# The second mixture of experts on four experts at a time, and the place of its spill branch

## The chip, the cores and the metric

The program runs on one core of a Trainium2 chip: TensorE (matrix products, PE in the profile), VectorE (DVE), ScalarE (ACT), GpSimd (POOL) and SyncE (SP), which issues most DMAs; 16 DMA engines move the data. The metric is the device time of one execution in microseconds (us); the median of several runs counts.

## The reference, cut to what matters

A two-layer backbone over 256 latent and 256 context tokens of 1024 values, all in float32. Layer 0 has a convolution and attention mixer, layer 1 a recurrent one (RG-LRU); each layer ends with a mixture of 16 experts in 4 groups. In layer 1 only the latent tokens go on, so the second mixture has 256 tokens:

```python
def hier_moe(h, w_grp, b_grp, w_rt, b_rt, w_gate, w_up, w_down):
    g_logit = jnp.einsum('bsd,dg->bsg', h, w_grp, preferred_element_type=f32) + b_grp.astype(f32)
    p_grp = jax.nn.softmax(g_logit, axis=-1)
    g_idx = jnp.argmax(g_logit, axis=-1)
    ...
    top_v, top_i = lax.top_k(e_sel, TOP_K)                       # two of the four experts of the group
    w_sel = jax.nn.softmax(top_v, axis=-1) * p_sel
    ...
    hg = jnp.einsum('bsd,edf->bsef', h, w_gate)                  # 16 experts, 1024 -> 512
    hu = jnp.einsum('bsd,edf->bsef', h, w_up)
    act = jax.nn.silu(hg) * hu * gate[..., None].astype(h.dtype)
    return jnp.einsum('bsef,efd->bsd', act, w_down)              # 512 -> 1024, summed over the experts
```

Each token uses two experts, so the kernel multiplies an expert's weights only with the tokens that chose it.

## The kernel before

**Weights.** SBUF holds 23 buffers of 1 MiB, the units (`NU`). The list `todo` has all weight tiles (1,024 KB each) in the order of use; `load_ahead(n)` (L119) issues their DMAs on SyncE so that up to n tiles are loaded or loading ahead of use, as long as units are free; `wtile` takes the next tile, `used` gives its unit back. A unit given back goes to the end of a queue and the oldest is taken first; a DMA into it waits until the last reader of its old contents is done. An expert has six tiles: gate (`wg`) and up (`wu`) in two halves of the contraction, down (`wd`) in two halves of the outputs. `w_first` and `w_second` (L287, L292) append them for a list of experts. Both mixtures read all 16 experts: 96 tiles each.

**First mixture** (`moe0`, L997; 512 tokens). Groups of four experts are worked at once: `four` (L1098) holds the tokens of each expert as 32 stationary columns, so that four products of 32 columns stand side by side, and goes through `NR` = 3 parts of 32 slots. The rows come by indirect DMA (`fetch`) and go back by indirect DMA (`scatter`) into the DRAM tile `z`, except those of the last group, which stay on the chip (`yl`) and are placed by products with one-hots (`own`). The choice's weight is multiplied into the activations (L1150).

**Second mixture** (`moe1`, L1212; 256 tokens in two blocks of 128, each expert with 64 slots, `CAP1`). It works on eight pairs of experts. `first(pr)`: `slots_of` (L928) builds, for 2 x 64 slots, the one-hot `Sl` and the weighted one-hot `Sw` on VectorE; `gather_slots` (L945) multiplies the tokens with `Sl` (fp32, 16 products of 128 columns); `Sw` is transposed and split into two fp32r parts; `slots_by` (L891) multiplies with gate and up weights, 64 stationary columns per expert, two experts side by side; `act_of` makes the activations. `second(pr)`: four transposes of the activations, the down products, and for each half of the outputs and each token block three fp32r products with the split `Sw` (`mm3`, L176), which add into four PSUM banks `acc` over all pairs. Then the gated sum (`add_gated`, L534) and the store.

**Order.** The lines above give the program order. Within a window the scheduler of the framework moves an instruction forward on its engine when its inputs are ready by a cost model, so the trace shows for instance combining products of one pair among the down products. DMAs keep the order of SyncE's queue.

**Spill.** If more tokens choose an expert than it has slots, `spill_rounds` (L954) works them off in a loop inside a branch (`tc.If`) on a count `nri` made by `route`. With these inputs the count is zero, so its body isn't run, but each engine reads the count and branches, and nothing is scheduled across the branch. Its body names five to eight units. It stands behind the second group of the first mixture (L1177) and behind the fifth pair of the second (L1259). Before it `load_ahead(8)` keeps the number of loads lower, so that units are left for the body; behind it 12 or 13 are allowed again.

## Time and profile before

| | us |
|---|---|
| median of 3 runs | 1070.16 (1069.8 to 1070.17) |
| profiled execution | 1069.07 |
| its span, first to last instruction | 1067.3 |
| first mixture, first gate product to the last down product | 342.4 to about 605 |
| second mixture, first gate product to the end | 816.0 to 1067.3 |
| mean granted clock of TensorE over the span | 0.960 of 2.4 GHz |

All times in the views are from the start of the span. Busy times are sums over instructions, so an engine that is busy for all of a stretch may still be the one that is not waited for; the lists of waits say which.

### The profile page before, as it was taken

The numbers are of one execution on the slowest core, as the hardware profiler recorded it, in microseconds if no ns is written. First come the engines' busy times: TensorE is split into PE (matmuls) and PEld (weight loads), VectorE is DVE, ScalarE is ACT, GpSimd is POOL, SyncE is SP. The second block draws the span as 40 slices with busy tenths as digits, with TensorE's granted clock in tenths as the row PEclk, the third lists the DMA queues.
The fourth block names the chain that finished last, engine by engine and source line by source line (L and its number), as shares of the span: only waits on it lengthen the run. The fifth ranks groups of instructions, "written<-read, shape, count | busy, mean of one in ns | idle before, by whom it ended". The sixth has DMA issues, their size and how long they took to land. (4 is left out here: it accounts for less than half of the span.)

```text
span 1067.3 us, 15108 instructions
## 1 busy us (share of the span) xinstructions
PE 972.1 (91%) x6153; PEld 544.2 (51%) x6153; DVE 457.3 (43%) x957; ACT 269.6 (25%) x487; POOL 188.1 (18%) x152
## 2 busy tenths in 40 slices
PE   4699999999987999999999989888576999999997
PEld 2488657556876333333433478656363444443342
DVE  3756565567464020110202388798974111221112
ACT  3622433423121010000101254585721101100010
POOL 0244010031033011010010336467410000000000
PEclk9699999999997999999999999999777999999999
DMA  9934866879576899979999911242775999997941
GB/s 366 377 112 154 347 238 245 314 278 418 212 280 248 335 385 401 420 278 392 420 420 413 369 41 41 79 157 80 295 304 224 422 421 418 414 423 271 422 169 39
DMA packets 49548, 310.65 MB, mean 291 GB/s; under 512 B 7528, under 2 KB 8296, under 8 KB 14912
## 3 DMA queue, kind: packets, MB, share of 16 engines
q1 hardware_dynamic: 45648, 301.63, 71.0%
q0 software_dynamic: 3824, 7.99, 2.0%
q8 instruction: 50, 0.82, 0.3%
q14 instruction: 26, 0.21, 0.1%
HBM read 304.28 MB, written 9.50 MB: 294 GB/s over the span
## 5 line engine op out<-in xcount | busy, mean ns | idle before, releaser
L899 PE MATMUL ba<-w,hgT 128*64 128x512 f32 x512 | 112.7, 594 | 0.0
L178 PE MATMUL bz<-hT,wsp 128*128 128x256 f32 (+1 forms) x224 | 76.9, 345 | 0.0
L179 PE MATMUL bz<-hT,wsp 128*128 128x256 f32 (+1 forms) x224 | 74.5, 334 | 0.9 <-DVE hT L158 0.7
L180 PE MATMUL bz<-hT,wsp 128*128 128x256 f32 (+1 forms) x224 | 73.9, 331 | 0.0
L899 PEld LDWEIGHTS ba<-w,hgT 128*64 128x64 f32 x512 | 36.3, 137 | 70.0 <-issue 69.8
L899 PE MATMUL ba<-w,actT 128*64 128x512 f32 x256 | 66.9, 601 | 4.1 <-DVE actT L233 2.7
L1106 PE MATMUL bz<-w,hgT 128*32 128x512 f32 x512 | 61.4, 593 | 0.2 <-PEq L961 0.2
L155 ACT ACTIVATE wsp<-w 128x512 fp32r<-128x512 f32 (+1 forms) x64 | 46.5, 781 | 59.4 <-PE bz L180 17.4
L1106 PE MATMUL ba<-w,hgT 128*32 128x512 f32 x512 | 61.2, 592 | 0.0
L158 POOL TENSOR_TENSOR wsp<-w,wsp 128x512 fp32r<-128x512 f32 (+1 forms) x19 | 40.8, 2153 | 91.1 <-ACT wsp L155 81.5
L158 DVE TENSOR_TENSOR wsp<-w,wsp 128x512 fp32r<-128x512 f32 (+1 forms) x49 | 48.0, 1010 | 13.3 <-ACT wsp L155 13.0
L911 DVE TENSOR_TENSOR act<-ba,silu 128x512 f32<-128x512 f32 x8 | 5.5, 691 | 105.9 <-PE ba L899 105.9
L388 PE MATMUL bz<-w,sT 128*32 128x512 f32 x384 | 46.0, 604 | 3.8 <-DMA w<-in_ada_w_dram 3.8
L1340 DVE SCALAR_TENSOR_TENSOR uc<-u,ocw,uc 128x510 f32<-128x510 f32 (+2 forms) x48 | 44.5, 984 | 4.1 <-POOL uc L1338 4.0
L178 PEld LDWEIGHTS bz<-hT,wsp 128*128 128x128 f32 x224 | 42.1, 189 | 7.6 <-ACT wsp L155 3.3
L179 PEld LDWEIGHTS bz<-hT,wsp 128*128 128x128 f32 x224 | 42.3, 189 | 4.7 <-DVE hT L158 0.9
L1106 PE MATMUL ba<-w,actT 128*32 128x512 f32 x384 | 44.6, 593 | 0.0
L1106 PE MATMUL bz<-w,actT 128*32 128x512 f32 x384 | 44.4, 593 | 0.0
L180 PEld LDWEIGHTS bz<-hT,wsp 128*128 128x128 f32 x224 | 42.3, 189 | 3.6
L179 PE MATMUL bz<-wsp,hT 128*128 128x512 f32 x96 | 39.1, 407 | 3.4 <-DVE wsp L158 3.4
L873 ACT ACTIVATE ys<-ba 128x512 fp32r<-128x512 f32 (+1 forms) x24 | 12.6, 525 | 116.9 <-PE ba L899 107.9
L178 PE MATMUL bz<-wsp,hT 128*128 128x512 f32 x96 | 38.5, 408 | 2.4 <-ACT hT L155 2.4
(371 smaller groups left out, 1690.5 us busy)
## 6 DMA issues: line engine op xcount, KB each, us to landing
w<-in_wg_dram SPq DMA_DIRECT2D x64, 1024.0 KB, 11.4
w<-in_wu_dram SPq DMA_DIRECT2D x64, 1024.0 KB, 11.7
w<-in_wd_dram SPq DMA_DIRECT2D x64, 1024.0 KB, 11.1
w<-in_ada_w_dram SPq DMA_DIRECT2D x48, 1024.0 KB, 6.9
w<-in_od_w_in_dram SPq DMA_DIRECT2D x8, 1024.0 KB, 4.9
w<-in_w_qkv_dram SPq DMA_DIRECT2D x6, 1024.0 KB, 10.3
w<-in_w_conv_dram SPq DMA_DIRECT2D x6, 1024.0 KB, 7.8
w<-in_ev_w_out_dram SPq DMA_DIRECT2D x4, 1024.0 KB, 10.0
```

The costliest lines, as they stand in the source:

```text
L155: S.activation(hi, src, AF.Copy)
L158: (eng or lo_engine()).tensor_sub(lo, src, hi.bitcast(F))
L178: T.matmul(o, l[0], r[0], start=start, stop=False)
L179: T.matmul(o, l[0], r[1], start=False, stop=False)
L180: final[0] = T.matmul(o, l[1], r[0], start=False, stop=stop)
L388: T.matmul(m[32 * j:32 * j + 32], sT[:, k], w[:, j * 512:(j + 1) * 512], start=(k == 0), stop=(k == KD - 1), tile_position=(0, 32 * j))
L873: S.activation(dst[0], p, AF.Copy)
L899: T.matmul(o[i * n:(i + 1) * n], actT[:, k0 + k, i * n:(i + 1) * n], w[:, k], start=(k0 + k == 0), stop=(k0 + k == nk - 1))
L911: V.tensor_mul(t, up, s)
L1106: T.matmul(o[r][32 * j:32 * j + 32], actT[r][:, k0 + k, 32 * j:32 * j + 32], ws[j][:, k], start=(k0 + k == 0), stop=(k0 + k == nk - 1), ti ...
L1340: V.scalar_tensor_tensor(c[:, :, j:256], src[:, :, 0:256 - j], tap, c[:, :, j:256], op0=ALU.mult, op1=ALU.add)
```

## The change

The second mixture is rebuilt on the helpers of the first: `four`, the activations' transposes and the tables of slots (`slot_rows`) move out of `moe0` and take the number of parts as an argument. `moe1` now works on four groups of four experts, 32 columns each, in two parts (`NR1` = 2; 64 slots per expert as before). The tokens are split into two fp32r parts `hp` once (`in_parts`), and the gather of a group is 32 fp32r products of 256 columns with one-hots `S` (`rows_of`). The choice's weight goes into the activations (`tg`), so that the combining products use plain one-hots (`own`), which are one part: two products instead of three per part, half and block, and no transposes of `Sw`. The weights' order becomes four gate tiles, four gate, eight up, eight down per group. The combining products of a group's second half are issued behind the next group's gate products (`later`).

In both mixtures the spill branch moves behind the last group's up products and transposes, ahead of its down products; the `load_ahead(8)` and the return to 12 or 13 go. In `moe0` the one-hot for the first gather comes from `rows_of` instead of from `ats` and `gr`, and the load of the square-root table is tied to the last copy instead of the last SiLU. Small tiles are allocated by size so that both mixtures share them (`per_block`).

```diff
-SPILL0 = 1
-SPILL1 = 4
+NR1 = 2
+CAP1 = 32 * NR1
...
-    slot1 = cst.tile([128, 2, 64], F, name="slot1")
+    slot1 = cst.tile([128, 4, 32], F, name="slot1")
...
-    w_first(1, [0, 1])
-    for e in range(0, NE, 2):
-        if e < NE - 2:
-            w_first(1, [e + 2, e + 3])
-        w_second(1, [e, e + 1])
+    for q in range(4):
+        w_first(1, range(4 * q, 4 * q + 4))
+        w_second(1, range(4 * q, 4 * q + 4))
...
+    def rows_of(S, key, nb, q, rs, tmp):
+        for m, r in enumerate(rs):
+            V.tensor_scalar(tmp, key, -float(4 * q * BIG + 32 * r), None, op0=ALU.add)
+            for b in range(nb):
+                t = S[:, b, 128 * m:128 * m + 128]
+                V.tensor_scalar(t, slot1.rearrange("p a b -> p (a b)"), tmp[:, 0, b:b + 1], None, op0=ALU.is_equal)
+                V.scalar_tensor_tensor(t, slot1.rearrange("p a b -> p (a b)"), tmp[:, 1, b:b + 1], t.bitcast(F),
+                                       op0=ALU.is_equal, op1=ALU.add)
+
+    def four(place, nr, rows, nk, get):
+        o = [place([128, 512]) for _ in range(nr)]
+        for k0 in range(0, nk, 4):
+            ws = [get(j, k0) for j in range(4)]
+            for r in range(nr):
+                for k in range(4):
+                    for j in range(4):
+                        T.matmul(o[r][32 * j:32 * j + 32], rows(r, k0 + k)[:, 32 * j:32 * j + 32], ws[j][:, k],
+                                 start=(k0 + k == 0), stop=(k0 + k == nk - 1), tile_position=(0, 32 * j))
+            used(*ws)
+        return o
...
     def moe0(h2, ts, lg, rest, h2d):
...
+        rows_of(own, key, NT, 0, [0], view(small([128, 16], "ks"), [128, 2, NT]))
...
+            at = transposed_act(bank8, act)
             if q == 3:
+                spill_rounds(0, CAP0, NT, again, key, w, nri, empty)
                 give(hg01, hgT01, ys01)
...
-            if q == SPILL0 - 1:
-                load_ahead(8)
-            if q == SPILL0:
-                spill_rounds(0, CAP0, NT, again, key, w, nri, empty)
-                load_ahead(12)
-        warm(AF.Sqrt, silu[0])
+        warm(AF.Sqrt, final[1])
...
     def moe1(h2, ts, lg, rest):
         nb = 2
         load_ahead(13)
+        hp = [unit([128, 2, D], "hp", R) for _ in range(2)]
+        def in_parts(b):
+            for i in range(2):
+                c = slice(512 * i, 512 * i + 512)
+                split(hp[0][:, b, c], hp[1][:, b, c], h2[b][:, c], V)
+        in_parts(0)
         goh, ef, pos, key, w, nri = route(nb, lg, CAP1)
         rest()
+        in_parts(1)
+        give(*ts)
+        ks = view(small([128, 16], "ks"), [128, 2, nb])
+        hgT = unit([128, KD, 256], "hgT")
+        def gather(q):
+            S = piece([128, nb, 256], "S", R)
+            rows_of(S, key, nb, q, range(NR1), ks)
+            for k in range(0, KD, 2):
+                p = bank([128, 2, 256])
+                for i in range(2):
+                    for b in range(nb):
+                        for m, h in enumerate(hp):
+                            T.matmul(p[:, i], h[:, b, (k + i) * 128:(k + i + 1) * 128], S[:, b],
+                                     start=(b + m == 0), stop=(b + m == nb))
+                evict(hgT[:, k:k + 2], p)
+        gather(0)
+        tp = slot_rows(nb, NR1, goh, ef, pos, w)
...
+        def add(q, h, own, y):
+            for b in range(nb):
+                for n in range(2 * NR1):
+                    T.matmul(acc[b][h], own[:, n // 2, b], y[:, n // 2, n % 2],
+                             start=(q + n == 0), stop=(q == 3 and n == 2 * NR1 - 1))
+        later = lambda: None
+        for q in range(4):
+            g = four(bank, NR1, rows, KD, lambda j, k0: wtile(("wg", 1, 4 * q + j, k0)))
+            later()
+            sl = [piece([128, 512], "silu") for _ in range(NR1)]
+            for r in range(NR1):
+                S.activation(sl[r], g[r], AF.Silu)
+            u = four(bank, NR1, rows, KD, lambda j, k0: wtile(("wu", 1, 4 * q + j, k0)))
+            act = [piece([128, 512], "act") for _ in range(NR1)]
+            for r in range(NR1):
+                n = NR1 * q + r
+                V.scalar_tensor_tensor(act[r], u[r], tg[:, n:n + 1], sl[r], op0=ALU.mult, op1=ALU.mult)
+            if q < 3:
+                gather(q + 1)
+            else:
+                gates = gate_rows(1, 5, 1)
+            at = transposed_act(bank, act)
+            if q == 3:
+                spill_rounds(1, CAP1, nb, whole, key, w, nri)
+            own = piece([128, NR1, nb, 128], "own", R)
...
+            yh = [ys, ys if q < 3 else unit([128, NR1, 2, 512], "ys", R)]
+            o = [None, None]
+            for h in range(2):
+                o[h] = four(bank, NR1, at, 4, lambda j, k0: wtile(("wd", 1, 4 * q + j, h)))
+                if h == 0:
+                    for r in range(NR1):
+                        put_parts((yh[0][:, r, 0], yh[0][:, r, 1]), o[0][r])
+            add(q, 0, own, yh[0])
+            for r in range(NR1):
+                put_parts((yh[1][:, r, 0], yh[1][:, r, 1]), o[1][r])
...
```

`slot_rows` is the code that stood in `moe0` (L1009 to L1039) with the number of blocks and parts as arguments; it fills `tp`, from which `tg` (the weight of each slot) and `last` (its token) come.

## Rows read from the trace of the kernel before

**Rows 1.** The page, its parts 1 and 2: busy time of TensorE (us, share of the span, instructions), then what the DMA engines moved in each of the 40 slices of 26.7 us, in GB/s.

```profile
PE 972.1 (91%) x6153; PEld 544.2 (51%) x6153; DVE 457.3 (43%) x957; ACT 269.6 (25%) x487; POOL 188.1 (18%) x152
...
GB/s 366 377 112 154 347 238 245 314 278 418 212 280 248 335 385 401 420 278 392 420 420 413 369 41 41 79 157 80 295 304 224 422 421 418 414 423 271 422 169 39
```

**Rows 2.** Busy time of each engine in the stretches of two pairs of experts of the second MoE (from one pair's first gate product to the next pair's): the stretch, its length, busy us and instructions of PE, PEld, DVE, ACT and POOL, granted TensorE clock, DMA share, GB/s. The second stretch holds the spill branch.

```profile
895.28:925.84 30.56, 29.87 (x147) 13.15 (x147) 5.91 (x16) 2.88 (x6) 0.00 (x0) 1.00 1.01 419
...
956.61:989.64 33.03, 30.73 (x147) 13.26 (x146) 6.30 (x18) 2.77 (x5) 0.00 (x0) 1.00 0.76 299
```

**Rows 3.** The same view in a stretch of 10 us near the end.

```profile
1030.00:1040.00 10.00, 9.72 (x47) 3.26 (x43) 0.69 (x1) 1.20 (x2) 0.00 (x0) 1.00 0.00 0
```

**Rows 4.** Who waited for whom between 816 and 1067 us: the longest wait of TensorE by total (total us, times, longest us).

```profile
PE bz L178 <- ACT ys L873: 3.2, 5, 0.7
```

**Rows 5.** TensorE's instructions in order of time (start us, us from the first start to the last end, engine, line, operation, names, shapes, count): gather products, gate and up products, and the down products of a pair with the combining products among them, until the next gather.

```profile
829.91 3.84 PE L951 MATMUL ba<-S,h 128*128 128x128 f32 x32
...
833.90 13.96 PE L899 MATMUL ba<-w,hgT 128*64 128x512 f32 x64
...
849.18 4.50 PE L899 MATMUL ba<-w,actT 128*64 128x512 f32 x18 [0.74 <-ACT actT L231]
853.61 0.73 PE L178 MATMUL bz<-ys 128*128 128x512 f32 x2
...
859.13 1.16 PE L951 MATMUL ba<-S,h 128*128 128x128 f32 x8
```

**Rows 6.** The same view in the first MoE: transposes of activations and the down products on 32 columns.

```profile
386.85 0.60 PE L1158 MATMUL ba<-ident,act 128*128 128x128 f32 x4
387.29 0.60 PE L1158 MATMUL bz<-ident,act 128*128 128x128 f32 x4
387.82 3.64 PE L1106 MATMUL ba<-w,actT 128*32 128x512 f32 x32
391.27 3.62 PE L1106 MATMUL bz<-w,actT 128*32 128x512 f32 x32
```

**Rows 7.** The same view: two fp32r products of 256 columns in the recurrent mixer, then two of 512 columns in its output projection.

```profile
690.14 0.28 PE L179 MATMUL bz<-hT,wsp 128*128 128x256 f32 x1
690.26 0.28 PE L180 MATMUL bz<-hT,wsp 128*128 128x256 f32 x1
...
788.06 0.39 PE L179 MATMUL ba<-wsp,mixT 128*128 128x512 f32 x1
788.29 0.40 PE L180 MATMUL ba<-wsp,mixT 128*128 128x512 f32 x1
```

**Rows 8.** The DMA queue of SyncE in order of time (issues of the second MoE's weights, 1,024 KB each), and from the view of the DMA queues the gates' loads (KB each, median us from issue to landing).

```profile
793.76 11.12 SPq L126 DMA_DIRECT2D w<-in_wd_dram  x3
...
820.13 6.77 SPq L126 DMA_DIRECT2D w<-in_wg_dram  x4
...
971.33 4.60 SPq L126 DMA_DIRECT2D w<-in_wd_dram  x4
...
gates<-rows SPq DMA_DIRECT2D x6, 512.0 KB, 14.3
```

**Rows 9.** Busy time and clock in stretches of 5 us around the second MoE's first products (columns as in rows 2).

```profile
810.00:815.00 5.00, 4.53 (x26) 4.50 (x27) 4.09 (x18) 0.81 (x2) 0.00 (x0) 0.62 0.04 16
...
820.00:825.00 5.00, 5.00 (x26) 1.68 (x24) 0.00 (x0) 0.60 (x1) 0.00 (x0) 1.00 0.85 316
```

**Rows 10.** All engines in order of time at that place: the last operation on `key`, the first one-hot comparison, the first of 32 gather products, the first gate products.

```profile
808.95 0.16 DVE L858 SCALAR_TENSOR_TENSOR key<-key,pos 128x4 f32<-128x4 f32 x1
...
809.15 0.28 DVE L938 TENSOR_SCALAR S<-slot,key 128x128 f32<-128x128 f32 x1
...
810.74 1.16 PE L951 MATMUL ba<-S,h 128*128 128x128 f32 x4
...
816.03 13.96 PE L899 MATMUL ba<-w,hgT 128*64 128x512 f32 x64
```

**Rows 11.** All engines in order of time at the end: the last down products, and the subtraction that makes the second part of their result.

```profile
1056.33 2.79 PE L899 MATMUL ba<-w,actT 128*64 128x512 f32 x10
...
1059.79 0.69 DVE L874 TENSOR_TENSOR ys<-ba,ys 128x512 fp32r<-128x512 f32 x1 [1.33 <-ACT ys L873]
```

**Rows 12.** Two groups of four experts of the first MoE (columns as in rows 2; the second begins right behind its spill branch), and from the waits of SyncE's queue its own time at the branch lines.

```profile
408.44:474.46 66.02, 66.02 (x617) 23.80 (x609) 6.93 (x10) 6.57 (x11) 6.01 (x6) 1.00 0.92 382
474.46:541.67 67.21, 67.06 (x617) 25.28 (x616) 7.79 (x11) 5.97 (x10) 2.92 (x3) 1.00 0.96 391
...
SPq L961 <- SPq L961: 6.0, 4, 3.7
```

**Rows 13.** All engines in order of time at the end of the first MoE: reads of the scattered rows, their sums on GpSimd, the first product that needs one.

```profile
583.10 4.34 SPq L1191 DMA_DIRECT2D zb<-z  x8
...
589.91 10.03 POOL L1194 TENSOR_TENSOR zb<-zb 128x512 f32<-128x512 f32 x8 [46.07 <-DMA zb<-z]
...
607.03 1.02 PE L1204 MATMUL ba<-zb,ident 128*128 128x512 f32 x2
```

**Rows 14.** The modulation products at the start of the kernel, in order of time, and the busy time and clock of a stretch of 5 us there (columns as in rows 2).

```profile
26.91 1.06 PE L388 MATMUL bz<-w,sT 128*32 128x512 f32 x8 [1.41 <-DMA w<-in_ada_w_dram]
29.41 1.93 PE L388 MATMUL bz<-w,sT 128*32 128x512 f32 x8 [1.43 <-DMA w<-in_ada_w_dram]
...
30.00:35.00 5.00, 2.43 (x12) 0.71 (x4) 2.30 (x13) 2.06 (x4) 0.00 (x0) 0.50 0.80 214
```

More of the change, by code (lines that the diff above doesn't have):

```diff
@@ L997, in moe0, with transposed_act @@
+    def transposed_act(place, act):
+        at = [piece([128, 4, 128], "actT") for _ in act]
+        for t, c in zip(at, act):
+            p = place([128, 4, 128])
+            for k in range(4):
+                T.transpose(p[:, k], c[:, k * 128:(k + 1) * 128], ident)
+            evict(t, p)
+        return lambda r, k: at[r][:, k]
     def moe0(h2, ts, lg, rest, h2d):
@@ L1130, in moe0 @@
             rows_T(r)
-        last = small([128, NR, NT], "last")
+        last = view(small([128, 16], "last"), [128, NR, NT])
         for r in range(NR):
@@ L1141, in moe0 @@
                     fetch(q + 1, r)
-            g = four(hgT, KD, lambda j, k0: wtile(("wg", 0, 4 * q + j, k0)))
+            g = four(bank8, NR, lambda r, k: hgT[r][:, k], KD, lambda j, k0: wtile(("wg", 0, 4 * q + j, k0)))
             sl = [piece([128, 512], "silu") for _ in range(NR)]
@@ new lines, in moe1, with whole @@
+        gather(0)
+        tp = slot_rows(nb, NR1, goh, ef, pos, w)
+        last = view(small([128, 16], "last"), [128, 4 * NR1, nb])
+        tg = small([128, 16], "tg")[:, 0:4 * NR1]
+        for b in range(nb):
+            V.tensor_scalar(last[:, :, b], tp[:, :, 0], float(BIG - 128 * b), None, op0=ALU.add)
+        V.tensor_copy(tg, tp[:, :, 2])
+        ys = unit([128, NR1, 2, 512], "ys", R)
+        acc = [[bank([128, 512], "z") for _ in range(2)] for _ in range(nb)]
+        def whole():
+            t = unit([128, 2, D], "h2")
+            for b in range(nb):
+                V.tensor_add(t[:, b], hp[0][:, b].bitcast(F), hp[1][:, b].bitcast(F))
+            return [t[:, b] for b in range(nb)], [t]
@@ new lines, in rows, with later @@
+        def rows(r, k):
+            return hgT[:, k, 128 * r:128 * r + 128]
+        def add(q, h, own, y):
+            for b in range(nb):
+                for n in range(2 * NR1):
[22 more added lines that the diff above has]
+            for r in range(NR1):
+                for b in range(nb):
+                    n = NR1 * q + r
+                    V.tensor_scalar(own[:, r, b], slot0, last[:, n, b:b + 1], None, op0=ALU.is_equal)
+            yh = [ys, ys if q < 3 else unit([128, NR1, 2, 512], "ys", R)]
[6 more added lines that the diff above has]
+            add(q, 0, own, yh[0])
+            for r in range(NR1):
+                put_parts((yh[1][:, r, 0], yh[1][:, r, 1]), o[1][r])
+            def later(q=q, own=own, y=yh[1]):
+                add(q, 1, own, y)
@@ L1263, in decay_rates @@
+        for h in range(2):
+            if h:
+                later()
+            hs = slice(h * 512, (h + 1) * 512)
+            for b in range(nb):
+                add_gated(b, h, acc[b][h], gates[:, 0])
+                nc.sync.dma_start(out[0, b * 128:(b + 1) * 128, hs], xb(b)[:, hs])
     def decay_rates(after):
```

157 lines of the change are left out of this document (52 added, 105 removed).

## The prediction

> **What bounds the kernel now.** The page first [rows 1]: TensorE is busy for 91% of the span, and in the second MoE (slices 32 to 40) the DMA engines move about 420 GB/s in nearly every slice, so two resources look full. Which of them sets the pace is read from three views. One pair of experts takes 30.6 us, of which TensorE is busy for 29.9 [rows 2]. A pair's weights are 12 tiles of 1,024 KB (1.049 MB); at the 419 GB/s of that row a tile takes 2.50 us, the same that lies between two products that wait for their tiles at the start of the kernel (26.91 to 29.41) [rows 14], and a pair 30.0 us. So the two are within 2% of each other, but the waits decide: no wait of TensorE on a transfer stands in the list, its longest is 3.2 us on ScalarE [rows 4]. The DMA engines rest three times in this stage: before the first weights come free (0.04 busy at 810 to 815) [rows 9], around the spill branch (0.76 over that pair) [rows 2], and at the end: from 1030 on nothing is moved while TensorE still multiplies for 30 us [rows 3, 11]. TensorE is the bound; the transfers would be done earlier.
>
> **The order of products, counted.** An fp32 product is two instructions. Now, a pair's gate and up products are 64 instructions on 64 columns and take 13.9 us [rows 5], so 27.8 for two pairs. After, a group's four experts are 128 + 128 instructions on 32 columns, and the first MoE has just this form: 32 instructions every 3.44 us [rows 6], 8 x 3.44 = 27.5. So the columns themselves gain nothing (the slots are the same 64 per expert, in two parts of 32). The down half is 128 instructions, 13.8 us for the group; now it takes 849.18 to 859.13 = 9.95 us for a pair with six combining products in it [rows 5]. At 0.218 us an instruction and 0.23 a combining product [rows 7] these are 32 x 0.218 + 6 x 0.23 = 8.4; the 1.6 left over, with five changes between 64 columns and 128, are 0.3 for each change. In the first MoE, four transpose instructions take 0.44 (386.85 to 387.29), and the first products on 32 columns begin 0.53 after the last four, so the change costs about 0.1 there [rows 6]. [...]
>
> What is gained lies beside the weights. Gather: now 32 instructions in 3.84 us per pair [rows 5], 7.7 for two; after, 32 fp32r products of 256 columns per group at 0.12 us [rows 7] = 3.8. Combining: now 3 products for each half and token block, 24 per group's two pairs at 0.23 = 5.5; after 16, 3.7. The transposes of the weighted one-hots (two per pair) go; those of the activations stay, 8 x 0.11 = 0.9 [rows 6]. A group of the new form on TensorE: 27.5 + 13.8 + 3.8 + 0.9 + 3.7 + 0.7 for the copied activations (as the 0.74 in rows 5) + six changes at 0.1 to 0.3 = 51.0 to 52.2 us. I take 52, against 61.2 now. Its 24 tiles take 60.0 us to come. So **the transfers become the bound** of this stage, and the sum goes along them.
>
> **The sum.** Start of the first gate product, 816.0 now [rows 10]. Added before it: the two subtractions that split the second token block, 0.69 each [rows 11], on VectorE between the router's small operations, 0 to 1.4 (the first block's are a step earlier, where VectorE has gaps; 0 to 1.4 again): I take 1.4. The gather now begins 1.6 us after the first comparison, with one block's one-hots (809.15 to 810.74); after, it needs both parts and blocks, ten operations at 0.2, 2.1: +0.5. The 32 gather products are at 1.2 GHz at first both times (clock 0.62 in 810 to 815) [rows 9]; 0 to +2, and less the two transposes that lay among them, I take 0. `slot_rows` (some 15 small operations on VectorE, 8 short instructions on TensorE) can stand behind the gather or behind the first weights: 0 to 1.5, I take 0.6. So 818.5, between 816.5 and 821.
>
> By then 18 tiles are loaded: 23 units less x, two parts of h2, hgT and ys (19 are issued now: the last before 820 begins in the row 793.76, with one more unit free) [rows 8]. The first four come free after two parts of 32 instructions, 6.9 us: 825.4. Now the first comes free at 820.13, and the stretch 820 to 825 moves 316 x 5 / 419 = 3.8 us worth of bytes, so 1.1 us pass until it moves [rows 8, 9]: 826.5. The remaining 78 tiles x 2.50 = 195.0: 1021.5. No hole is left in them: a tile needs the unit of the tile 18 before it, and TensorE, at 52 us a group against 60, frees units ahead of need; the spill branch is crossed by SyncE behind the last weight. The last four tiles' products 6.9: 1028.4. Then what follows the last down product now, 1056.33 + 2.79 to the span's end at 1067.3, 8.2 us [rows 11] (copies, four combining products, the gated sum, the stores; the same but for one copy more that runs beside products): 1036.6. The gates' load (512 KB, 1.25 us) [rows 8] is queued behind the last weights and needed 7 us later: 0. TensorE's own path ends its last down product at 818.5 + 3 x 52 + 27.5 + 2.3 + 13.8 + 1 for the branch = 1019.1, 9 us earlier, so it is covered; that cover is gone at 55 us a group.
>
> **The first MoE.** `slot_rows` is the same code with one operation more, and `own` comes from `key` rather than from the one-hots, nine small operations for eight: 0, within 0.5. The moved branch: a group takes 66.0 us, the one behind the branch 67.2 [rows 12], so about 1.2 us of TensorE go at the old place and come back at the new one, between the activations' transposes and the last down products; bounds -1.2 (if a wait there hides it) and +2.5 (SyncE's longest time at a branch is 3.7 [rows 12]; were TensorE's as long). I take 0. Its loads (gates, rows, the experts' weights by index) are not issued when no expert overflows. What is queued behind it: on SyncE the gates, the reads of z and the mixer's first weights, on GpSimd the sums of z, on VectorE the one-hots for the last group. The units that the branch's body names come free only when all engines are past it, at about 585; the reads of z are issued at 583.1, the sums end at 599.9 and the first product that needs one is at 607.0 [rows 13], so some 5 us cover a delay of 2 to 3. The mixer's weights may come 2 to 3 us later too, and another rotation of the units can move single loads there: -1 to +4 in all, taken as 0. The loads no longer held back at that branch bring nothing: TensorE waits for no weight in either group (66.02 busy of 66.02) [rows 12].
>
> So a span of 1036.6. The profiled execution took 1069.07 for a span of 1067.3, 1.8 more, and the median of the runs is 1.1 above it: 1039.5, set down as **1040 us**, 2.8% less.
>
> **The rivals.** (a) TensorE stays the bound. If the adds, gathers and transposes are woven into the weights' products as the combining products are now (five changes for each down half) [rows 5], at 0.3 us each, with waits for PSUM copies, a group may take 57 us: 818.5 + 171 + 49 + 8.2 = 1046.7, so 1050. For it: half of the 0.3 per change is unexplained; against it: in the first MoE the same helper ran with 66.02 busy of 66.02. Chance 0.13.
> (b) The change does not do what it should, as the transfers set the pace already (420 GB/s over most of the stage [rows 1]); then only the hole at the branch is won, 33.0 - 30.6 = 2.4 us on TensorE [rows 2], to 9 us on the transfers: 1061 to 1068. Against it: TensorE never waits for a tile [rows 4], and 30 us of products follow the last transfer [rows 3]. Chance 0.05.
> (c) Slower, by TensorE's clock. Where it waits for weights in the modulation, 1.06 us of products for each tile of 2.5 us, the clock falls to 0.50 of 2.4 GHz, that is 1.2 [rows 14]. After the change TensorE catches up with the transfers in the last group and then does 6.9 us of products for each 10.0 of transfers. If it fell there and stayed, four tiles would take 13.8: the last group, begun at 974.5, ends at 974.5 + 6 x 13.8 + 4 + 9.5 = 1070.8, so 1074. That is the point from which it is slower than now: one whole group at 1.2 GHz. Against it: in both MoEs the clock stays at 1.00, short waits included [rows 2, 12]. Chance 0.03. [...]
>
> **How the numbers follow.** The forecast has 0.79. Its own range: the start -2 to +2.5, the first MoE and mixer -1 to +4, the tile time at 2.48 rather than 2.50 -1.5: 1035 to 1046. The range of 1034 to 1052 adds a microsecond below and takes in (a), up to a group of 57.5; it leaves out (b), (c) and the far end of (a). A change within 0.2% (2 us, about what a measurement of this kernel can tell from none) needs (b) at its far end: 0.02. Slower: (c), 0.03. Faster: 0.95.
>
> **What would show it.** Right: waits of TensorE on `w` DMAs in the last group or two, none before; a DMA share near 1.0 from about 826 to 1021 without a hole; 32 instructions every 3.44 us in the second MoE; some 15 us from the last landing to the end. Wrong: DMA idle for long before the end means (a); a clock under 1.0 in the last 60 us means (c); a first gate product later than 821, or z(0) of the mixer later than now, would mis-size the start.

## The result, and the profile after

The changed kernel takes 1045.47 us (median of 4 runs, 1045.24 to 1046.01) where the kernel before takes 1069.98 beside it (4 runs): ratio 0.9776, interval 0.9759 to 0.9793, 24.5 us. Forecast were 1040 and a range of 1034 to 1052. The profiled execution has a span of 1043.5 us, 6.9 more than the 1036.6 of the sum. The first MoE and the mixer end where they did (VectorE takes up the second MoE's norm at 789.89, at 789.97 before), so all of it lies behind them.

The page shows the change of bound at a glance. From slice 33 on the DMA engines' GB/s stay above 420, and fall only in the last two slices (of 26.1 us), where before the last 30 us are idle [rows 1, 3]; TensorE is busy for 948.5 us instead of 972.1:

```profile
PE 948.5 (91%) x6753; PEld 528.6 (51%) x6753; DVE 455.0 (44%) x948; ACT 271.9 (26%) x485; POOL 188.2 (18%) x152
...
GB/s 367 379 101 181 310 236 304 300 232 414 308 182 283 285 388 397 422 411 416 421 363 408 237 250 40 121 81 81 201 233 295 155 422 421 421 421 421 421 388 195
```

The start of the second MoE: TensorE's instructions in order of time, and VectorE's added subtractions, of the first token block (797.04) and the second (columns as in [rows 5]). The first gate product is at 820.00, not 816.03 [rows 10]:

```profile
813.76 5.50 PE L1253 MATMUL ba<-S,hp 128*128 128x256 f32 x32 [3.35 <-DVE S L1039]
819.10 0.97 PE L1028 MATMUL ba<-of,at 128*128 128x24 f32 x8
820.00 27.67 PE L1050 MATMUL ba<-w,hgT 128*32 128x512 f32 x256
```

```profile
797.04 1.29 DVE L157 TENSOR_TENSOR hp<-h,hp 128x512 fp32r<-128x512 f32 x2
799.29 0.69 DVE L232 COPY x2T<-bz 128x512 f32<-128x512 f32 x1 [0.95 <-PE bz L760]
...
807.28 0.69 DVE L157 TENSOR_TENSOR hp<-h,hp 128x512 fp32r<-128x512 f32 x1
...
808.06 0.68 DVE L157 TENSOR_TENSOR hp<-h,hp 128x512 fp32r<-128x512 f32 x1
```

The last group on TensorE, from its first gate product on. 248 gate and up instructions take 980.15 to 1013.45, 33.3 us (eight more stand among the down products before them, from 975.5), where the first group has 256 in 27.7. The brackets show waits for up tiles, two of them under the name of SyncE's branch. By the times at which tiles land (below), TensorE follows the landings from 993.97 on: tiles land at 993.93, 996.41, 1003.87 and 1006.35, and their first products start at 993.97, 996.46, 1003.91 and 1006.40. The row of four in 1.90 us is the one expert whose tile landed at 1003.87: products of one expert alone start 0.43 apart, where those of four experts in turn take 3.44 for 32 [rows 6]. The last up tile is the one used at 1006.40. From there TensorE waits for no weights until its 1.10 at the branch. The last row of 56 down products takes 8.0 us, where it takes 7.2 without the branch (e1); the last tile lands within it, at 1027.77, and is used at 1027.82:

```profile
980.15 15.73 PE L1050 MATMUL ba<-w,hgT 128*32 128x512 f32 x132
996.46 7.09 PE L1050 MATMUL ba<-w,hgT 128*32 128x512 f32 x60 [0.58 <-DMA w<-in_wu_dram]
1003.91 1.90 PE L1050 MATMUL ba<-w,hgT 128*32 128x512 f32 x4 [0.36 <-SPq L963]
1006.40 7.05 PE L1050 MATMUL ba<-w,hgT 128*32 128x512 f32 x52 [0.58 <-SPq L963]
...
1016.12 8.78 PE L1050 MATMUL ba<-w,actT 128*32 128x512 f32 x72 [1.10 <-DVEq L963]
1024.83 2.12 PE L1280 MATMUL bz<-ys,own 128*128 128x512 f32 x8
1026.88 7.99 PE L1050 MATMUL ba<-w,actT 128*32 128x512 f32 x56
1034.80 2.21 PE L1280 MATMUL bz<-ys,own 128*128 128x512 f32 x8
```

The transfers: the DMA queue of SyncE in order of time, then busy times and DMA share by stretch (columns as in [rows 2]). SyncE issues eight tiles every 19.9 us, 2.49 each, and the engines move 421 GB/s from 830 to 1010; then comes a hole, in which 1012 to 1017 move 2.1 us' worth too little. SyncE issues the last eight down tiles in 27 us instead of 18: it spends 16.6 us at the branch, of which the list of waits tells:

```profile
888.19 17.73 SPq L125 DMA_DIRECT2D w<-in_wg_dram  x8
908.08 17.72 SPq L125 DMA_DIRECT2D w<-in_wu_dram  x8
...
988.92 27.07 SPq L125 DMA_DIRECT2D w<-in_wd_dram  x8
1016.08 0.95 SPq L432 DMA_DIRECT2D gates<-rows  x1
```

```profile
830.00:1010.00 180.00, 177.27 (x1472) 70.68 (x1468) 26.77 (x62) 17.23 (x29) 0.00 (x0) 1.00 1.01 421
...
1012.00:1013.00 1.00, 1.00 (x4) 0.22 (x2) 0.00 (x0) 0.00 (x0) 0.00 (x0) 1.00 0.71 295
1013.00:1014.00 1.00, 1.00 (x6) 0.42 (x4) 0.44 (x1) 0.00 (x0) 0.00 (x0) 1.00 0.51 213
1014.00:1015.00 1.00, 0.67 (x5) 0.42 (x4) 0.31 (x1) 0.60 (x1) 0.00 (x0) 1.00 0.37 123
1015.00:1016.00 1.00, 0.02 (x1) 0.00 (x0) 0.69 (x1) 0.00 (x0) 0.00 (x0) 1.00 1.06 254
1016.00:1017.00 1.00, 0.88 (x9) 0.50 (x12) 0.00 (x0) 0.00 (x0) 0.00 (x0) 1.00 0.86 352
```

```profile
SPq L963 <- SPq L963: 16.6, 7, 2.6
```

In the program as built, SyncE's queue has the branch ahead of the last four down tiles, although they were requested earlier in the kernel's text, and behind its comparison of the count, at 997.2, SyncE waits seven times, each time for one of the eight loads in flight; the last of these lands at 1013.9 and the next load is issued at 1014.0. So the last four are asked for when the engines have run empty.

A measure for what follows. The runs of one kernel differ by 1 to 2 us, and the profiles show most of that ahead of the router. The stage itself, from the first weight product to the end of the span, repeats within 0.5 us, so it is read by three marks of each profile: the first weight product, the first use of the last up tile where TensorE waits for it (as the row 1006.40 above), the end of the span.

| profile | first weight product | to the last up tile | from there to the end | stage | median us | ratio to before, interval |
|---|---|---|---|---|---|---|
| changed | 820.00 | 186.4 | 37.1 | 223.5 | 1045.47 | 0.9776, 0.9759 to 0.9793 |
| e5 changed again | 820.91 | 186.4 | 36.7 | 223.1 | 1044.57 | 0.9776, 0.9762 to 0.9789 |
| e1 no branch | 817.63 | 186.3 | 35.0 | 221.3 | 1042.32 | 0.9763, 0.9749 to 0.9776 |
| e2 late count | 818.28 | 186.5 | 37.4 | 223.8 | 1045.47 | 0.9787, 0.9773 to 0.9800 |
| e3 split on GpSimd | 821.39 | 186.4 | 36.9 | 223.3 | 1046.34 | 0.9791, 0.9777 to 0.9804 |
| e4 one more tile | 818.85 | 184.7 | 37.5 | 222.2 | 1042.81 | 0.9764, 0.9749 to 0.9778 |
| e6 fewer weights | 820.32 | no wait | | 211.3 | 1032.14 | 0.9662, 0.9648 to 0.9675 |
| e7 gather once | 819.29 | 186.2 | 36.9 | 223.1 | 1045.11 | 0.9788, 0.9775 to 0.9802 |
| e8 branches moved only | 816.70 | | | 256.6 | 1074.93 | 1.0056, 1.0042 to 1.0070 |
| e9 branch in the middle | 819.64 | no wait | | 224.4 | 1045.81 | 0.9784, 0.9771 to 0.9798 |
| e10 loads first | 820.89 | 186.3 | 36.1 | 222.4 | 1043.86 | 0.9768, 0.9754 to 0.9781 |
| e11 and one more tile | 820.26 | 184.3 | 35.6 | 219.8 | 1041.92 | 0.9753, 0.9739 to 0.9766 |
| e12 tile by tile | 819.63 | 185.9 | 50.3 | 236.2 | 1057.93 | 0.9896, 0.9881 to 0.9911 |

The same measure for the kernel before is 1067.3 - 816.0 = 251.3.

### The profile page after: what moved, and what is told of

Same layout as the page of the kernel before. It is cut to its first block, busy times and chain, and to the rows that moved or that the text cites. A ratio compares the mean times of both kernels' runs of the same rounds, so it can differ in the third digit from the quotient of the medians.

```text
span 1043.5 us, 16277 instructions
## 1 busy us (share of the span) xinstructions
PE 948.5 (91%) x6753; PEld 528.6 (51%) x6753; DVE 455.0 (44%) x948; ACT 271.9 (26%) x485; POOL 188.2 (18%) x152
## 3 DMA queue, kind: packets, MB, share of 16 engines
q0 software_dynamic: 3824, 7.99, 2.1%
## 5 line engine op out<-in xcount | busy, mean ns | idle before, releaser
L1050 PE MATMUL ba<-w,hgT 128*32 128x512 f32 x1536 | 178.9, 593 | 1.5 <-SPq L963 0.9
L1050 PEld LDWEIGHTS ba<-w,hgT 128*32 128x32 f32 x1536 | 53.7, 110 | 116.1 <-issue 110.2
L1050 PE MATMUL ba<-w,actT 128*32 128x512 f32 x896 | 108.5, 593 | 1.9 <-DVEq L963 1.1
L1050 PEld LDWEIGHTS ba<-w,actT 128*32 128x32 f32 x896 | 38.0, 110 | 62.6 <-issue 58.0
L1050 PE MATMUL bz<-w,hgT 128*32 128x512 f32 x512 | 58.0, 592 | 0.0
L1294 DVE SCALAR_TENSOR_TENSOR act<-ba,tg,silu 128x512 f32<-128x512 f32 x8 | 6.0, 751 | 90.2 <-PE ba L1050 90.2
L178 PE MATMUL bz<-wsp,hT 128*128 128x512 f32 x96 | 39.1, 407 | 3.4 <-DVE wsp L157 3.4
L1173 DVE SCALAR_TENSOR_TENSOR act<-bz,tg,silu 128x512 f32<-128x512 f32 x6 | 4.5, 750 | 85.1 <-PE bz L1050 85.1
L177 PE MATMUL bz<-wsp,hT 128*128 128x512 f32 x96 | 38.5, 408 | 2.4 <-ACT hT L154 2.4
L179 PE MATMUL bz<-wsp,hT 128*128 128x512 f32 x96 | 38.8, 405 | 0.0
## 6 DMA issues: line engine op xcount, KB each, us to landing
w<-in_wu_dram SPq DMA_DIRECT2D x64, 1024.0 KB, 12.4
```

The costliest lines, as they stand in the source:

```text
L177: T.matmul(o, l[0], r[0], start=start, stop=False)
L178: T.matmul(o, l[0], r[1], start=False, stop=False)
L179: final[0] = T.matmul(o, l[1], r[0], start=False, stop=stop)
L1050: T.matmul(o[r][32 * j:32 * j + 32], rows(r, k0 + k)[:, 32 * j:32 * j + 32], ws[j][:, k], start=(k0 + k == 0), stop=(k0 + k == nk - 1), ti ...
L1173: V.scalar_tensor_tensor(act[r], u[r], tg[:, n:n + 1], sl[r], op0=ALU.mult, op1=ALU.mult)
L1294: V.scalar_tensor_tensor(act[r], u[r], tg[:, n:n + 1], sl[r], op0=ALU.mult, op1=ALU.mult)
```

## The experiments

Two theories stand against each other for the bound: transfers set the pace of the second MoE now, or TensorE still does (rival a of the prediction). Within the first, the question is what the 6.9 us are made of.

**e6: a sixth of the weights not loaded, the products kept.**

```diff
-        for h in range(2):
+        for h in range(2 - l):
...
+            wd = []
...
-                o[h] = four(bank, NR1, at, 4, lambda j, k0: wtile(("wd", 1, 4 * q + j, h)))
+                if h == 0:
+                    o[h] = four(bank, NR1, at, 4, lambda j, k0: wtile(("wd", 1, 4 * q + j, 0)), lambda *ws: wd.extend(ws))
+                else:
+                    o[h] = four(bank, NR1, at, 4, lambda j, k0: wd[j])
```

> The 16 tiles of the second down halves of the second MoE are not loaded; the first halves are used twice, so that half of the down projection's result is other numbers, with the same products on TensorE. Theory, transfers set the pace: all waits of TensorE on weights in the last group go (5.6 us in its gate and up products, 1.8 and 0.9 us in its down products, by their excess over the first group's 27.7 and 13.9 us), the branch's 1.1 us on TensorE stays, and the time falls by 7 to 9 us, to 1036 to 1038, where TensorE's own path is the bound. Rival, TensorE's own products set the end as in the kernel before: no change (within 0.5 us).

12.4 us faster than the changed kernel beside it (1032.14 against 1044.57), as the theory of the transfers has it and not the rival; but it won 4 us more than its expectation had. The reason is that the edit also changes the order in which the scheduler places the products. The second group's up products in the changed kernel again (e5; a part of the next gather stands between) and in this run:

```profile
885.54 8.78 PE L1050 MATMUL ba<-w,hgT 128*32 128x512 f32 x76
...
896.10 7.05 PE L1050 MATMUL ba<-w,hgT 128*32 128x512 f32 x52
```

```profile
884.95 13.94 PE L1050 MATMUL ba<-w,hgT 128*32 128x512 f32 x128
```

The same 128 instructions take 15.83 us in the one and 13.94 in the other. No weights are waited for in either: in e5 the last up tile of this group lands at 886.52 and is first used at 896.10. And e6, which waits for no weights at all, has the very same two rows in its last group, where combining products stand between:

```profile
971.38 8.78 PE L1050 MATMUL ba<-w,hgT 128*32 128x512 f32 x76
...
981.23 7.05 PE L1050 MATMUL ba<-w,hgT 128*32 128x512 f32 x52
```

So the 1.9 us are the order: where a row is cut in two, three or four products of one expert stand alone at its ends, 0.43 apart. Groups 2 and 3 have most of such cuts in the changed kernel (868.70 to 980.15) and few here (869.02 to 971.38); without the products that lie in one stretch only, the changed kernel's order costs there some 6 us more, an estimate from the rows. From the first weight product to the end of the last down product this run takes 201.4 us (1021.70 - 820.32); the forecast had 200.6 for TensorE's own path. In the changed kernel's order that path would be some 207.5, still short of the 214.9 (1034.87 - 820.00) that it takes. By itself e6 doesn't part the weights left out from the new order; the next run does.

**e7: less work for TensorE, the transfers kept.** `gather(q + 1)` is left out.

> Groups 1 to 3 use the gathered tokens of group 0, so that their experts get other tokens' rows: three gathers (3 x 4.0 us of TensorE) and their one-hots are left out, and no transfer changes. Theory, transfers set the pace: within 1 us of the changed kernel, TensorE's waits on weights some 12 us longer. Rival, TensorE sets the pace: 12 us faster, about 1033.

The stage takes 223.1 us, as in the changed kernel: 12 us of products less are worth nothing, so a better order of the products can't have been worth anything either as long as the tiles come as they do. With e6 this settles the bound from both sides.

**e5: the changed kernel again.**

> The changed kernel once more, beside the next three and on their chip, since the runs without the branch differ by 1 to 2 us among themselves in the stretch ahead of the second MoE. Expected by all theories: 223.5 us from the first weight product to the end of the span (1043.5 - 820.0), as the first profile had it, within 0.5 us, whatever the stretch ahead of it takes; total 1044 to 1046.

223.1 us, as expected.

**e1: no branch in the second MoE.** `spill_rounds(1, ...)` is left out.

> The second MoE's spill branch is left out (with these inputs its rounds are not run anyway), so nothing stands between the weight requests on SyncE's queue. Theory, transfers set the end: the last four down tiles are requested as soon as their buffers are free (about 997 instead of 1014), the share of the DMA engines stays near 1.0 to the last tile (no fall to 0.6 to 0.7 at 1012 to 1016), about 2 us won there, and the time falls by 2 to 3.5 us, to about 1042.5. Rival, TensorE's own products set the end: only the 1.1 us that TensorE loses at the branch go, and the time falls by about 1 us. Second rival, the branch costs nothing that counts: within 0.5 us.

By the medians 1042.32, and 2.0 us less in the stage than the mean of the changed kernel's two profiles (223.3). All of it lies behind the last up tile, 35.0 us instead of 36.7 to 37.1: no 1.10 between transposes and down products (the last transposes end at 1012.51), and a last row of down products of 7.16 instead of 7.99. Here TensorE and the last tile come together: the tile lands at 1023.86.

```profile
1011.85 0.66 PE L1060 MATMUL ba<-ident,act 128*128 128x128 f32 x4 [0.33 <-DVE act L1294]
1012.44 8.78 PE L1050 MATMUL ba<-w,actT 128*32 128x512 f32 x72
...
1023.80 7.16 PE L1050 MATMUL ba<-w,actT 128*32 128x512 f32 x56
1030.89 2.21 PE L1280 MATMUL bz<-ys,own 128*128 128x512 f32 x8
```

**e2 and e10: the branch kept, the loads ahead of it.** The count that the branch reads comes from a silu tile of the last group, so that on SyncE all loads are ready first. e10 also writes the first half's combining products ahead of the second half's down products.

```diff
+                late = small([128, 1], "late", I32)
+                V.scalar_tensor_tensor(late, sl[0][:, 0:1], 0.0, nri, op0=ALU.mult, op1=ALU.add)
-                spill_rounds(1, CAP1, nb, whole, key, w, nri)
+                spill_rounds(1, CAP1, nb, whole, key, w, late)
```

> The branch stays where it is, but the count that it loads is made from a silu tile of the last group, so that SyncE's queue has all eight last down tiles and the gates' rows ahead of the branch. Theory, the order on SyncE's queue made the hole and put the gates' 512 KB among the last tiles: DMA share 1.0 to the last tile, gates landing behind the last weight, and the time falls by 2.5 to 3.5 us, though TensorE still crosses the branch. Rival, TensorE's crossing of the branch (1.1 us) is what costs: within 0.5 us of the changed kernel.

> As the run with the late count (all loads and the gates' rows stand ahead of the branch on SyncE's queue), and the first half's combining products of the last group are written ahead of the second half's down products, where TensorE had them in the changed kernel. Theory, the hole at the branch costs 2 us of transfers and the run with the late count gave them back by TensorE's order: 221 to 222 us from the first weight product to the end instead of 223.3. Rival, the hole costs nothing and the run without the branch won only TensorE's crossing: 223.3 again.

e2 is a miss: 223.8, no gain. The hole is gone (0.99 to 1.04 of DMA share from 1000 to 1016), but the scheduler placed TensorE's 16 last combining products behind all down products; now it idles for 1.40 before the last half, until the last tile lands at 1024.55, and does them all at the end:

```profile
1014.47 8.72 PE L1050 MATMUL ba<-w,actT 128*32 128x512 f32 x70 [1.11 <-DVEq L963]
1024.59 7.05 PE L1050 MATMUL ba<-w,actT 128*32 128x512 f32 x58 [1.40 <-SPq L963]
1031.57 3.96 PE L1280 MATMUL bz<-ys,own 128*128 128x512 f32 x16
```

e10 has the order back: 222.4, and 36.1 behind the last up tile. That is 1.1 more than without the branch, TensorE's crossing of it (1.11 in its list of waits), and 0.6 to 1.0 less than the changed kernel. So the hole costs 0.6 to 1.0 (with what a slightly other order of the last products does), not the 2 us that the expectation had, since the products of the first half cover most of it.

**e4 and e11: one more tile in place.** The unit `ys` is claimed behind the first gate products.

```diff
-        ys = unit([128, NR1, 2, 512], "ys", R)
...
+            if q == 0:                           # behind four() of the gate weights
+                ys = unit([128, NR1, 2, 512], "ys", R)
```

> The buffer for the expert outputs is claimed behind the first gate products instead of ahead of them, so that 19 weight tiles instead of 18 are in place at the first product. Theory, transfers set the end from the first release on: one tile fewer behind it, 2.5 us sooner, 1043.0. Rival, TensorE sets the end: no change (within 0.5 us).

> The previous kernel with one more tile in place at the first product (the expert outputs' buffer claimed later). Theory, transfers set the end: 1.3 to 2.5 us less again, 219 to 220.5 us from the first weight product to the end, and a time of 1040 to 1042. Rival, TensorE's own path (205 us to its last product and 6 us of tail by the run with fewer weights) or the order of its last products stops it: no more than 0.5 us.

To the last up tile they take 1.7 and 2.1 us less than the 186.4 of the others (a tile is 2.49), so a tile fewer behind the first release is worth most of its time up to there. Over the whole stage e4 wins 1.1 us (222.2 against 223.3), e11 2.6 (against e10). e11, with both edits and the branch kept, is the best version found here: 219.8 us of stage, ratio 0.9753 against 0.9776; the intervals overlap, the stage is 3.5 us shorter.

**e3: the small parts of the second token block on GpSimd.**

```diff
-                split(hp[0][:, b, c], hp[1][:, b, c], h2[b][:, c], V)
+                split(hp[0][:, b, c], hp[1][:, b, c], h2[b][:, c], (V, G)[b])
```

> The two subtractions that make the small parts of the second block of tokens (2 x 0.69 us of VectorE amid the router's chain) are on GpSimd. Theory: the first weight product starts 1.0 to 1.4 us sooner (820.0 to about 818.8), the first release of buffers follows it, and since transfers set the end the time falls by the same 1.0 to 1.4 us. Rival: GpSimd's subtractions end late (1.6 to 1.8 us each by its additions in the same stretch), the gather waits for them or VectorE is slowed beside them, and the start moves by less than 0.5 us, either way.

The theory fails, and so does the rival's bound of 0.5 us, though the slower VectorE that it names is seen. From the last product of the logits to the first weight product it takes 22.0 us (799.39 to 821.39) instead of 20.0 (800.03 to 820.00). The router's product waits 9.01 for VectorE instead of 8.20, 0.8 of it. The other 1.2 lie in the gather: its 32 products take 6.74 us instead of 5.50. In the changed kernel TensorE's granted clock is 0.50 until 817, 0.91 in 817 to 818 and 1.00 behind it, and these products start 0.214 us apart until 817.1 and 0.114 apart from 817.3 on. By an estimate from these distances, all but the last few products of this run are at the slow pace, so the clock rises at about 820 here. Why it rises later is not shown. In VectorE's order of time two small operations of the router, 0.17 and 0.21 us in the changed kernel, take 1.00 and 1.24, while GpSimd does its subtractions:

```profile
805.10 1.00 DVE L810 TENSOR_TENSOR goh<-slot,gf 128x8 f32<-128x8 f32 x1
806.14 1.24 DVE L826 TENSOR_TENSOR et<-lg,goh 128x32 f32<-128x32 f32 x1
```

```profile
804.81 2.51 POOL L157 TENSOR_TENSOR hp<-h,hp 128x512 fp32r<-128x512 f32 x2
```

That is 0.8 to 1.0 us more for each of these two. In the changed kernel, too, one small operation of this chain is as long, while GpSimd does its addition (803.67 to 805.49): L808 takes 1.25 us at 804.27 and 0.17 at 806.80. Others run beside GpSimd and are no longer than elsewhere (L809 takes 0.16 at 804.91 in e3), and what tells the long ones from the short is not shown.

**e8 and e9: the branch's place by itself.** e8 is the kernel before with both branches moved; e9 the changed kernel with the second branch back behind group 1 (`load_ahead(8)` behind group 0, 13 behind the branch).

> The kernel before, in pairs of experts, with nothing changed but the place of the two spill branches (behind the last up products of either MoE, no narrowing of the loads ahead of them). Theory, the new place of the branches alone is worth 0 to 2.5 us (the pair that held the second branch took 33.03 us where others took 30.56) and the rest of the 24.5 us is the new order of the products: 1066 to 1068 where the kernel before takes 1068.2. Rival, the branches in the middle held much of it back by the halt of the transfers: 8 us or more faster.

> The changed kernel with the second MoE's branch back in the middle, as the kernel before had it: the loads ahead narrowed from 13 to 8 behind group 0, the branch behind group 1, then 13 again. Theory, transfers set the pace now, so the halt that the branch brings (about 8 us of transfers in the pair that held it in the kernel before) is lost in full: 6 to 9 us slower than the changed kernel, 229 to 232 us from the first weight product to the end of the span instead of 223.3. Rival, the halt is made up by the buffers' depth: within 2.5 us, the price that the branch had for TensorE in the kernel before.

In e8 both the theory and its rival fail; in e9 the theory fails and the rival (within 2.5 us) holds. Alone, the move makes the kernel before 6.2 us slower (1074.93 against 1068.76). The loss lies in the pairs from which the branch was taken: from the gate products of the sixth pair to the end of the last pair's, busy times by stretch, before and e8.

```profile
957.00:1034.00 77.00, 73.80 (x356) 30.73 (x352) 11.77 (x33) 6.72 (x13) 0.00 (x0) 1.00 0.78 318
```

```profile
957.70:1040.50 82.80, 77.90 (x360) 31.68 (x358) 11.42 (x31) 7.33 (x14) 0.00 (x0) 1.00 0.74 295
```

82.8 us instead of 77.0, with 4.9 instead of 3.2 in which TensorE is not busy. With no branch to stop at, the scheduler weaves the next gather's products in groups of some four to sixteen among the gate products and puts the down products right behind; TensorE then waits eight times, 0.2 to 0.9 each, for activations and copies. What the rest of the 5.8 is (changes of form inside the busy time, transfers at 276 GB/s in 990 to 1000) stays open.

In the changed form the old place costs 1.1 us of the stage (224.4 against 223.3), not 6 to 9. TensorE stands still for 5.45 us there, eight products behind the branch ("issue": it waits for nothing that the profile shows, so the cause is not shown), and runs at 0.50 of its clock for the next stretch; but the transfers lose only some 2 us (376 and 374 GB/s in 910 to 930), as SyncE's eight loads in flight last through most of the halt, and the last group's gate and up products come without a wait, 27.68 us for 248 of them:

```profile
925.08 1.91 PE L1050 MATMUL ba<-w,hgT 128*32 128x512 f32 x8 [0.30 <-PEq L963]
932.43 1.22 PE L1280 MATMUL bz<-ys,own 128*128 128x512 f32 x2 [5.45 <-issue]
...
988.76 27.68 PE L1050 MATMUL ba<-w,hgT 128*32 128x512 f32 x248
```

```profile
910.00:920.00 10.00, 10.00 (x78) 4.24 (x74) 1.38 (x2) 1.16 (x2) 0.00 (x0) 1.00 0.95 376
920.00:930.00 10.00, 6.69 (x38) 2.38 (x30) 3.56 (x11) 1.20 (x2) 0.00 (x0) 0.98 0.97 374
...
932.00:934.00 2.00, 1.56 (x6) 0.71 (x10) 0.00 (x0) 0.00 (x0) 0.00 (x0) 0.50 1.01 426
934.00:936.00 2.00, 2.00 (x12) 0.38 (x8) 0.00 (x0) 0.00 (x0) 0.00 (x0) 0.50 1.01 426
936.00:938.00 2.00, 2.00 (x21) 0.64 (x17) 0.00 (x0) 0.00 (x0) 0.00 (x0) 0.91 1.01 414
```

**e12: the last four down tiles one after the other.** Loops j, r, k instead of r, k, j for the last half.

> The previous kernel with the last four down tiles worked through one after the other, so that a tile's products start when it has landed, where the changed kernel turns from expert to expert (column group to column group) with every product and starts when all four are there. If a 32-column product takes its 0.107 us in any order, the last products end up to 4 us sooner. If the four experts' products share the time because they run beside each other in their column groups, the 32 instructions of this half take up to four times their 6.9 us, and the time grows by 10 to 20 us.

TensorE's row of these products in e12 and in e11:

```profile
1025.85 21.74 PE L1319 MATMUL ba<-w,actT 128*32 128x512 f32 x62
```

```profile
1024.80 7.07 PE L1050 MATMUL ba<-w,actT 128*32 128x512 f32 x62
```

0.35 us for an instruction instead of 0.11, 14.7 us in this row, and no wait for a tile in it (the last lands at 1025.50): the order of the four experts' products alone makes the row 3.1 times as long. Where they alternate, the four start together (996.46 to 996.48 and again 996.91 to 996.93 in the changed kernel).

## Why the prediction was right, and where its sum was short

Right: the bound went over to the transfers (e6, e7), at 2.49 us a tile (2.50 forecast), and rival (a) was no case: TensorE's own path is 201.4 us to the last down product in e6's order (200.6 forecast) and some 207.5 in the changed kernel's, a group 50.9 to 51.5 without waits in e6 (52). The price of a change between 64 or 128 columns and 32, 0.1 to 0.3 us in the sum, was an estimate from [rows 5, 6]; no run parts it from the rest of a group. Rival (b) is out by the result, rival (c) by the clock, 1.00 in the rows from 826 to 1035. The sign "waits of TensorE on `w` DMAs in the last group or two, none before" came true: the first use that follows a landing is at 993.97, in the last group. The gates' load was rightly counted at nothing: VectorE waits 4.2 us for it, but for a sum that is done at 1031, six us before the last one. The first MoE's part was 0, as taken, and by the way that was forecast: the products behind the branch's old place start 1.1 us sooner (519.96, before 521.04), and the last down product ends at 605.59 in both.

Short: the span by 6.9 us, in four places.

- **Start of the first gate product**, 818.5 forecast, 820.0 measured: +1.5. The first block's subtractions were taken at 0, but VectorE does them ahead of the second block's copy, 799.29 instead of 798.33: 1.0. The second block's lengthen the wait for the router's product from 7.14 to 8.20: 1.1 (1.4 taken). From there to the gather it is 3.6 instead of 2.4 us, the one-hots: 1.3 (0.5), and from the gather's start to the first gate product 6.2 instead of 5.6, `slot_rows`: 0.7 (0.6).
- **"1.1 us pass until it moves"**: the first release is 7.1 us behind the first product (6.9), and by the bytes moved in 828 to 830 (172 and 393 GB/s) the transfers begin at 828.65, 1.6 behind it: +0.7 together; 70 tiles at 2.49 instead of 2.50 give 0.7 back.
- **A tile counted as landed when its bytes were.** 828.65 + 70 x 2.49 = 1003.0 is when the 88th tile, the last up tile, should be there; TensorE uses it at 1006.40, +3.4. It is no wait of TensorE's: the view of the issuing line shows that tile issued at 986.4 and landed 19.9 later, 1006.3.

```profile
L125 SPq DMA_DIRECT2D w<-in_wu_dram x2: 327/327/327, 984.0 to 986.4; - x2
...
DMA to landing us min/median/max: 19.9/19.9/19.9
```

Each load has 16 semaphore steps in the trace, and where TensorE waits for a tile its first product on it starts 0.04 to 0.05 us behind the last step. The 88th tile's first step is at 1002.90, as the sum by bytes has it, five are done by 1002.95, thirteen by 1004.90, and the last three come at 1006.25 to 1006.35. So the loads come in line, 2.49 apart, and the 3.4 us are the spread of one load's steps: three come far behind the others. The spread is 0.5 us at the first load of the stage, 1.8 at the second, at most 2.0 until the load that lands at 952.74, 3.3 to 3.6 from the one that lands at 956.72 to the one at 1016.36, and 2.0 again for the last four, behind the hole. At the stage's first releases the view of the issuing line has the first load landed at 832.0 (issued 827.1) and the next at 835.8 (827.5):

```profile
L125 SPq DMA_DIRECT2D w<-in_wd_dram x2: 328/356/383, 827.1 to 827.5; - x2
...
DMA to landing us min/median/max: 4.9/6.6/8.3
```

I had taken 1.1 us from the bytes of the kernel before and no more, as there TensorE never waited for a landing. That is the largest term. In e1, e2, e3 and e10 the last up tile is used 3.0 to 3.5 us behind the same sum, an estimate from the bytes moved in 826 to 832 (e10: 820 to 830) and 2.49 a tile. Both jumps of the spread stand right behind a fetch of 16 KB in the queue that the page calls instruction (832.98 and 954.54, 0.9 and 1.1 us long), but ten more such fetches between 845 and 1006 come without a jump, so the cause is not shown.
- **"No hole is left in them: ... the spill branch is crossed by SyncE behind the last weight"** failed. The branch stands ahead of the last four, and there is a hole of 2.1 us of transfers. It costs 0.6 to 1.0 (e10). The other 1.1 is TensorE's own crossing (e10 against e1): the sum had it on TensorE's covered path alone, but behind the last up tile nothing covers it. Without the branch TensorE comes to the last tile just as that lands (1023.80 and 1023.86); with the loads first and the branch kept, the tile is there at 1027.26 and TensorE comes at 1027.62. From the last up tile to the end the sum has 1036.6 - 1001.5 = 35.1 us; without branch it takes 35.0, and that is no luck, as its parts agree too: eight landings in 20.0 (20.0 forecast), 7.1 (6.9) and 8.0 (8.2). Now it takes 37.1: +2.0.

1.5 + 0.7 - 0.7 + 3.4 + 2.0 = 6.9.

The time still lies in the sum's own range of 1035 to 1046, but in part by luck: the room was set aside for the start and the first MoE, and the landing and the end, 5.4 us together, had none. And rival (b)'s price for the moved branches alone, 2.4 to 9 us won, is not borne out: in the old order they lose 6.2 us (e8), and in the new one the place of the second MoE's branch wins 1.1 (e9).

## What to carry to other kernels

When a change hands the bound from TensorE to the transfers, sum along the landing of the last tile that TensorE can't go on without, look up how far that landing is behind its bytes (3.4 us here, after 174 us of transfers at 421 GB/s), and add what TensorE does behind it. A runtime branch whose body is not run was still a wall here, 16.6 us on SyncE's queue: look where it stands on the queue that issues the loads, for what was requested earlier in the text can stand behind it. An edit priced on the old order of instructions may have the other sign on the new one (the branch's place, 6.2 us lost in e8 and 1.1 won by e9), so time the parts on both. And before a longer row of products is called a wait, look for the same row in a run that can't wait: e6 shows that it was their order.

## What the runs showed of the hardware

- Products on 32 columns take 0.11 us each in a row of four experts (e11, 62 in 7.07 us) and 0.35 when one expert's follow each other (e12, 62 in 21.74), 3.1 times as much; where one expert's products stand alone, they start 0.43 apart (last group of the changed kernel).
- TensorE's clock: after 5.45 us without a product it was 0.50 of full speed from 932 to 936, 0.91 in 936 to 938 and 1.00 from 938 on (e9); the waits of the last group, of at most 1.10 us in its rows, left it at 1.00 (changed kernel). At 0.50 the gather's products of 256 columns start 0.214 us apart, at 1.00 0.114 (changed kernel, 814 to 819).
- Two small operations of VectorE, 0.17 and 0.21 us in the changed kernel, took 1.00 and 1.24 us while GpSimd did its subtractions (e3).
- A load's 16 semaphore steps don't come together: 0.5 us lie between the first and the last at the stage's first load and 3.3 to 3.6 from 956.72 to 1016.36 (changed kernel). Where TensorE waited for a tile, its first product on it started 0.04 to 0.05 us behind the last step (993.93 and 993.97, 1006.35 and 1006.40).
- At the branch SyncE waits for the loads in flight, 16.6 us, though the branch's body is not run (changed kernel); TensorE's crossing there is 1.1 us (e10 against e1).
